# A hybrid decoder layer on one Trainium2 core: the memory branch's norms and roundings are moved into the gates, branch A's first weights are asked for earlier, and softmax scaling goes from VectorE to GpSimd

## The chip, the cores and the metric

One core of one Trainium2 chip runs the whole kernel as one program. Its engines are TensorE (PE, with its weight load PEld), VectorE (DVE), ScalarE (ACT), GpSimd (POOL) and SyncE (SP), which here issues the DMAs. The metric is device microseconds per execution. Lower is better.

## What is computed

One layer of a decoder: a feed-forward block, a mixer of three branches, and a second feed-forward block, on 1024 tokens of width 1024 in f32. Cut to the mixer:

```python
h = rmsnorm(x, mix_norm[l])
z = h @ w_in[l]
u = jax.nn.gelu(z[..., COL_U:COL_V], approximate=False)
v = jax.nn.gelu(z[..., COL_V:COL_CQ], approximate=False)
y_a = spatial_gating(u, v, sg_ln_g[l], sg_ln_b[l], sg_w[l], sg_b[l])
y_b = mla(...)
y_c = memory_attention(z[..., COL_QM:COL_GATE], mem, ...)
gates = jax.nn.sigmoid(z[..., COL_GATE:] + b_gate[l]).reshape(B, S, N_BRANCH, D_MODEL)
merged = (gates[:, :, 0] * (y_a @ w_branch_a[l])
          + gates[:, :, 1] * (y_b @ w_branch_b[l])
          + gates[:, :, 2] * (y_c @ w_branch_c[l]))
...
def memory_attention(q_m, mem, mem_norm, w_kv, q_norm, k_norm):
    q = rmsnorm(q_m.reshape(B, S, MEM_HEADS, MEM_HEAD_DIM), q_norm)
    kv = rmsnorm(mem, mem_norm) @ w_kv
    ...
    s = jnp.einsum('bshd,bmhd->bhsm', q, k).astype(jnp.float32) * (MEM_HEAD_DIM ** -0.5)
    p = jax.nn.softmax(s, axis=-1)
    return jnp.einsum('bhsm,bmhd->bshd', p.astype(v.dtype), v).reshape(B, S, MEM_WIDTH)
```

The memory has 256 rows and the branch has 4 heads of width 128.

## The kernel before

Every f32 operand of a matmul is stored as two parts, `hi` (rounded to fp32r, by ACT) and `lo` (the rest, by DVE): `split` (L129), or `split_gain` (L138) with a gain. A product is three matmuls, hi x hi, hi x lo and lo x hi: `mm3` (L144), whose lines L147 to L149 stand for nearly all of PE's work.

The stages run in this order: feed-forward 1, the gates, the mixer, feed-forward 2. Feed-forward and gates form their products with seven multiplications of half blocks in place of eight. In the gates, `Gates.run` (L1538) goes over units f = 3 to 13. A unit (`unit_steps`, L1338) fetches 1 MB of weights, makes four sums of them on DVE (L1305), splits them (L135, L136) and runs seven products of 12 matmuls. Its four results go through `emit` (L1521): units 0 to 11 give 24 sigmoid gates, units 12 and 13 the four heads of the memory branch's queries, unrounded, and each goes to DRAM from a `raw` buffer.

The mixer is `latent` and `qkv` (branch B's inputs), then `sgu` (L614, branch A up to its projection), then `mem_kv` (L719) and `mem_attention` (L781) of branch C. Inside `sgu`, for the second half of the tokens, `mem_norm` (L690) loads, norms and splits the memory rows between the steps of the U product, and `mem_queries` (L750) loads the four heads into `raw` buffers, squares them (L764), splits them with their gain and leaves the sums over squares (L774) for later. `branches` (L552) is a generator: each step multiplies one 128-column block of branch A's projection for half of the tokens. Its steps serve as filler for PE: three before the first product of `mem_kv`, two before the second, and the rest between the steps of `mem_attention`, where `scores` (S), `turn` (T, transposes) and `value` (V) of eight query tiles follow each other. `scores` ends in minimum, Exp, reciprocal and a scaling on DVE (L806).

What sets the order: in blocks marked `manual_schedule` the named engines keep the written order of the block's instructions. All else is ordered at build time by a list scheduler that simulates the engines: it issues what is ready, with the written order as priority, so work that depends on little is placed early. After that the order of each engine is fixed. In `Gates.run` only PE is named; in `sgu`, `mem_kv` and `mem_attention` no engine is. Buffers come from rings of fixed size by tag, and an instruction that writes a new tile needs a free one: `raw` 3, `whi` and `wlo` 5 each, `h` (`h4`) 16, `x` (`x4`) 10, `w4` 11, `t` (rows) 6; in PSUM `bank` 4, `one` 4 in the gates, `mm` 2 in the mixer. DMAs leave SP's queue in order. In the mixer the sixteen `h4` tiles hold the normed input h until the U products are done.

Of the kernel before, what the change touches and what calls it, by code (L numbers as in the profile page):

```python
# [8 lines left out]
F32 = mybir.dt.float32  # L9
# [7 lines left out]
P = 128  # L17
# [28 lines left out]
class Kernel:  # L46
# [551 lines left out]
    def gelu_rows(self, dst, h, w, pairs, amid={}):  # L598


        gelu = lambda d, x: self.nc.scalar.activation(d, x, ACT.Gelu)
        ps = [self.mm() for _ in range(2)] if pairs else [self.bank() for _ in range(4)]
        for d in range(DT):
            then = amid[d]() if d in amid else None
            for i in range(4):
                b = ps[i // 2][:, i % 2] if pairs else ps[i]
                first = self.mm3(b, tuple(x[:, i * P:(i + 1) * P] for x in h[d]), w[d], d == 0, d == DT - 1)
                if then:
                    self.after(first, then)
                then = None  # L610
        for i, b in enumerate(ps):
            gelu(dst[:, 2 * i:2 * i + 2] if pairs else dst[:, i], b)

    def sgu(self, h):  # L614
        nc, a, tc = self.nc, self.a, self.tc
        with tc.tile_pool(name="sgu", bufs=1) as p:
# [12 lines left out]
            for hf in range(2):  # L629
                vhi, vlo = (p.tile([P, 4, SGW], F32R, name=n, bufs=2) for n in ("v_hi", "v_lo"))  # L630
# [41 lines left out]
        return yt, next(mem), queries  # L672
# [17 lines left out]
    def mem_norm(self):  # L690
# [3 lines left out]
        views = lambda ts: [t[:, i].rearrange("p (c m) -> p c m", m=ML)[:, c]  # L694
                            for t in ts for i in range(2) for c in range(2)]
        x4 = [self.h4() for _ in range(2)]
        x = views(x4)
        for n, t in enumerate(x4):
# [3 lines left out]
        for n in range(4):  # L702
            acc = self.norm_feed(acc, x4[n // 2][:, n % 2], 512)
        nc.vector.tensor_tensor(acc[:, :ML], acc[:, :ML], acc[:, ML:], op=ALU.add)
        yield
        room = lambda: self.mm()[:, 0]
        ss = self.token_sums(acc[:, :ML], late=True, bank=room)
        last = self.final
        r = self.rms(ss, ML // P, D)
        yield last  # L710
        scale = self.norm_scale(r, late=True, bank=room)
        last = self.final
        hi, lo = (views([self.h4(F32R) for _ in range(2)]) for _ in range(2))
        for c in range(DT):
            self.norm_put(hi[c], lo[c], x[c], self.g_mem[:, c:c + 1], scale)
        yield last
        yield hi, lo

    def mem_kv(self, p, mt, fill, amid):  # L719
# [3 lines left out]
        kt = tuple(p.tile([P, MH, ML], F32R, name=n) for n in ("mk_hi", "mk_lo"))  # L723
        vv = tuple(p.tile([P, 2, MH * MD], F32R, name=n) for n in ("mv_hi", "mv_lo"))
# [12 lines left out]
        x = p.tile([P, 2, MH, MD], F32, name="m_k")  # L737
# [3 lines left out]
        amid()  # L741
# [8 lines left out]
    def mem_queries(self):  # L750


        nc = self.nc
        gq = self.stat("m_gq", 1)
        nc.gpsimd.tensor_scalar(gq, self.mq_g, -MD ** -0.5, None, op0=ALU.mult)
        qt, ss = [], []
        for pair in range(MH // 2):
            sq = [self.wide(n).bitcast(F32) for n in ("whi", "wlo")]
            for o in range(2):
                q = self.raw()  # L760
                nc.sync.dma_start(q, self.z[ZQ + 2 * pair + o].rearrange("p a w -> p (a w)"))
                qt.append(self.split_pair(self.h4))
                for n, t in enumerate(sq):
                    nc.scalar.activation(  # L764
                        t[o * P // 2:(o + 1) * P // 2], q[n * P // 2:(n + 1) * P // 2], ACT.Square)
                self.split_gain(*qt[-1], q, gq)
            nc.gpsimd.tensor_tensor(sq[0], sq[0], sq[1], op=ALU.add)
            ss.append(sq[0])
        yield
        b = self.bank()[:, :NT * MH]  # L770
        for pair, sq in enumerate(ss):
            for t in range(NT):
                at = t * MH + 2 * pair
                nc.tensor.matmul(b[:, at:at + 2], sq[:, t * P:(t + 1) * P], self.pick, start=True, stop=True)  # L774
        r = self.const.tile([P, NT * MH], F32, name="mq_r")
        nc.vector.tensor_copy(r, self.rms(b, NT * MH, MD))
        nr = self.const.tile([P, NT * MH], F32, name="mq_nr")
        nc.gpsimd.tensor_scalar(nr, r, -1.0, None, op0=ALU.mult)
        yield qt, r, nr

    def mem_attention(self, p, queries, kt, vv, filler):  # L781

        nc = self.nc
        qt, r, nr = queries
        st = {}

        def scores(i, k):
# [10 lines left out]
            pr = p.tile([P, MH, ML], F32, name="mpr", bufs=3)  # L798
# [7 lines left out]
            nc.vector.tensor_tensor(pr, pr, rs.unsqueeze(2).to_broadcast([P, MH, ML]), op=ALU.mult)  # L806
# [179 lines left out]
    def mixer(self, norm):  # L986
# [12 lines left out]
        ya, mt, queries = self.sgu(h)  # L999
# [9 lines left out]
        branch_a = self.branches(0, ya, sink_a)  # L1009
        with tc.tile_pool(name="mem", bufs=1) as p:  # L1010
            got = []
            kv = self.mem_kv(
                p, mt, lambda n: [next(branch_a) for _ in range(n)], lambda: got.append(next(queries)))
            yc = self.mem_attention(p, got[0], *kv, branch_a)
# [39 lines left out]
    def run(self):  # L1054
# [12 lines left out]
        with tc.tile_pool(name="f1", bufs=1) as fp, self.banks("f1ps") as self.pm:  # L1067
# [45 lines left out]
            self.sig = self.z = gates.z  # L1113
# [391 lines left out]
class Gates(Seven):  # L1505


    def __init__(self, k, w, pool, norm):
        super().__init__(k, w, pool, norm)
        self.z = [k.dram.tile([P, 2, 512], F32, name=f"gate{i}") for i in range(ZB)]  # L1510
        self.o, self.w0 = {}, {}
# [9 lines left out]
    def emit(self, f, i, half, row, ps, into=None):  # L1521
# [12 lines left out]
        o[1] += 1  # L1534
        if o[1] == 2:
            self.nc.sync.dma_start(self.z[n], self.o.pop(n)[0])

    def run(self, x1d, r0):  # L1538
# [3 lines left out]
        last = ZB // 2 - 1  # L1542
        E = mybir.EngineType
        with k.tc.manual_schedule(engines={E.PE}):
            for f in range(3, last + 1):
                self.fetch(f, [x4] * 4 if f % 2 else [x4, w4, x4, w4])
# [8 lines left out]
                self.unit(f)  # L1555
# [426 lines left out]
```

## Time and profile before

| what | value |
|---|---|
| median of 3 runs | 2214.19 us (2213.59 to 2215.88) |
| the profiled execution | 2213.92 us |
| its span, first to last instruction | 2212.1 us |
| mean granted clock of TensorE | 0.997 |
| DMA | 290.12 MB, mean 131 GB/s |
| the gates' units, about | 690 to 930 us of the span |
| `sgu`, about | 1056 to 1140 us |
| `mem_kv` and `mem_attention`, about | 1140 to 1250 us |

A row of groups reads: line of the code, engine, operation, output <- inputs by the program's names, shapes, count | busy us, mean ns of one | idle us of the engine before it and what ended that. A row of the timeline reads: start in us, length in us, engine, line, operation, names, shapes, count of merged instructions, and in brackets the idle time before it and what ended it. A line that is a helper's (L130, L131, L147) stands for many callers, so the tile names tell them apart. Matmul lengths overlap; what a matmul costs is the distance between two starts.

### The profile page before, as it was taken

Reading aid. Unit: us, or ns where it says so; the run is one execution under the profiler, and the core shown is the slowest. Engines: PE = TensorE matmul, PEld = TensorE weight load, DVE = VectorE, ACT = ScalarE, POOL = GpSimd, SP = SyncE. Lnnn points to the kernel's source line nnn. Section 1 sums busy time; section 2 is a strip of 40 time slices with the busy share of each in tenths; the row PEclk is TensorE's granted clock in tenths of the full one; section 3 lists DMA queues with packets and bytes.
Section 4 is the critical chain, followed back from the end, with each engine's and each line's share of the span. In section 5 each row is a group of like instructions: output and inputs, shape, how many; then the busy total and the mean of one; then the engine's idle time right before and its main releaser. Section 6 shows DMA issues by size and latency. Waiting matters only on the chain.

```text
span 2212.1 us, 27569 instructions
## 1 busy us (share of the span) xinstructions
PE 2182.9 (99%) x10280; PEld 1821.0 (82%) x10280; DVE 1548.5 (70%) x2386; ACT 902.0 (41%) x1489; POOL 262.8 (12%) x259
## 2 busy tenths in 40 slices
PE   9999999999999999999989999999999999999999
PEld 5888888888887888898878789988888888888887
DVE  7966666589888555538656668985886666657884
ACT  5422222243455433335435449843442222224332
POOL 2012121100000000003100131140011121210000
PEclk9999999999999999999999999999999999999999
DMA  4242322484432324314424550085032333338543
GB/s 144 81 153 99 103 99 100 162 305 147 148 110 95 115 101 147 110 51 153 129 86 157 211 199 30 30 294 200 29 114 101 100 114 100 115 108 298 174 129 105
DMA packets 114359, 290.12 MB, mean 131 GB/s; under 512 B 13488, under 2 KB 21808, under 8 KB 114224
## 3 DMA queue, kind: packets, MB, share of 16 engines
q1 hardware_dynamic: 114224, 288.36, 37.6%
q8 instruction: 81, 1.33, 0.2%
q14 instruction: 54, 0.44, 0.1%
HBM read 203.90 MB, written 84.41 MB: 130 GB/s over the span
## 4 chain that ended last, share of the span: by engine, by line
PE 89%; DVE 6%; ACT 2%; issue 1%; DMA 1%; POOL 0%; SPq 0%; ACTq 0%; DVEq 0%; POOLq 0%
PE one L147 13%; PE one L148 13%; PE one L149 13%; PE bank L147 13%; PE bank L148 12%; PE bank L149 12%; PE mm L147 2%; PE mm L148 2%; PE mm L149 2%; PE bank L926 1%; PE bank L941 1%; PE bank L942 1%; PE bank L425 1%; DVE wlo L136 1%; DVE wlo L131 1%
## 5 line engine op out<-in xcount | busy, mean ns | idle before, releaser
L135 ACT CAST whi<-x 128x1024 fp32r<-128x1024 f32 (+1 forms) x195 | 185.5, 953 | 489.7 <-PE one L148 215.5
L1332 DVE TENSOR_TENSOR t<-t,one 128x512 f32<-128x512 f32 x182 | 124.9, 686 | 236.3 <-PE one L149 236.1
L147 PE MATMUL bank<-h,whi 128*128 128x512 f32 x660 | 257.1, 390 | 0.0
L148 PE MATMUL bank<-h,whi 128*128 128x512 f32 x660 | 256.9, 389 | 0.0
L149 PE MATMUL bank<-h,wlo 128*128 128x512 f32 x660 | 256.8, 389 | 0.0
L136 DVE TENSOR_TENSOR wlo<-x,whi 128x1024 fp32r<-128x1024 f32 (+1 forms) x195 | 233.0, 1196 | 30.5 <-ACT whi L135 30.4
L147 PE MATMUL one<-h,whi 128*128 128x512 f32 x492 | 193.1, 393 | 0.0
L148 PE MATMUL one<-h,whi 128*128 128x512 f32 x492 | 192.0, 390 | 0.0
L149 PE MATMUL one<-h,wlo 128*128 128x512 f32 x492 | 192.0, 390 | 0.0
L147 PE MATMUL one<-w,whi 128*128 128x512 f32 x408 | 158.7, 389 | 0.0
L148 PE MATMUL one<-w,whi 128*128 128x512 f32 x408 | 158.7, 389 | 0.0
L149 PE MATMUL one<-w,wlo 128*128 128x512 f32 x408 | 158.7, 389 | 0.0
L1726 POOL TENSOR_TENSOR raw<-raw 128x512 f32<-128x512 f32 x38 | 63.0, 1658 | 789.5 <-DVE raw L1581 789.5
L130 ACT CAST whi<-w 128x1024 fp32r<-128x1024 f32 (+1 forms) x108 | 95.1, 899 | 143.9 <-PE one L148 55.2
L131 DVE TENSOR_TENSOR wlo<-w,whi 128x1024 fp32r<-128x1024 f32 (+1 forms) x108 | 110.1, 1033 | 60.5 <-ACT whi L130 60.4
L147 PEld LDWEIGHTS bank<-h,whi 128*128 128x128 f32 x660 | 123.9, 188 | 25.9 <-DVE h L131 0.4
L149 PEld LDWEIGHTS bank<-h,wlo 128*128 128x128 f32 x660 | 123.9, 188 | 25.7
L148 PEld LDWEIGHTS bank<-h,whi 128*128 128x128 f32 x660 | 123.9, 188 | 25.6
L147 PE MATMUL bank<-whi 128*128 128x512 f32 x352 | 136.9, 389 | 0.0
L148 PE MATMUL bank<-wlo,whi 128*128 128x512 f32 x352 | 136.9, 389 | 0.0
L149 PE MATMUL bank<-whi,wlo 128*128 128x512 f32 x352 | 136.9, 389 | 0.0
L148 PEld LDWEIGHTS one<-h,whi 128*128 128x128 f32 x492 | 92.8, 189 | 19.3 <-issue 0.2
(383 smaller groups left out, 4971.6 us busy)
## 6 DMA issues: line engine op xcount, KB each, us to landing
x<-in_ffn_w_gu_dram SPq DMA_DIRECT2D x78, 512.0 KB, 4.8
w<-tdt SPq DMA_DIRECT2D x40, 512.0 KB, 4.6
tdb<-raw SPq DMA_DIRECT2D x64, 256.0 KB, 2.1
h<-in_ffn_w_down_dram SPq DMA_DIRECT2D x64, 256.0 KB, 6.0
w<-tdb SPq DMA_DIRECT2D x30, 512.0 KB, 4.4
gate<-raw SPq DMA_DIRECT2D x27, 512.0 KB, 2.9
tdt<-w SPq DMA_DIRECT2D x48, 256.0 KB, 2.1
tdt<-raw SPq DMA_DIRECT2D x40, 256.0 KB, 2.7
```

What stands on the lines that cost most here:

```text
L130: self.nc.scalar.copy(hi, src)
L131: return (eng or self.nc.vector).tensor_tensor(lo, src, hi.bitcast(F32), op=ALU.subtract)
L135: self.nc.scalar.copy(hi, src)
L136: return lambda: self.nc.vector.tensor_tensor(lo, src, hi.bitcast(F32), op=ALU.subtract)
L147: i = mmul(out, s[0], m[0], start=first, stop=False, **kw)
L148: mmul(out, s[0], m[1], start=False, stop=False, **kw)
L149: self.last = mmul(out, s[1], m[0], start=False, stop=last, **kw)
L425: nc.tensor.transpose(b[:m, k * P:(k + 1) * P], s, self.ident)
L926: nc.tensor.transpose(b[:, at:at + P], prs[t][:, kk * P:(kk + 1) * P], self.ident)
L941: nc.tensor.matmul(o, w, pt[0], start=n == 0, stop=False)
L1332: return self.nc.vector.tensor_tensor(out, x, y, op=ALU.add)
L1726: sub = lambda d, x, y: (eng or nc.gpsimd).tensor_tensor(d, x, y, op=ALU.subtract)
```

## The change

Six edits go together:

1. In `emit`, a query head no longer goes to DRAM as it is. Each finished half is squared into two rows by `fold` (two heads share 128 partitions; the second head's call adds the two rows on GpSimd), and a finished head is split with its gain and stored as two parts, `hi` and `lo`, 512 KB each.
2. `Gates.run` takes the query units 12 and 13 right after unit 4. The sums over squares (`picked`) stand behind the first product of the two units after them, and the inverse roots `mq_r` and `mq_nr` are made at the end of the second.
3. `mem_norm` runs in three steps inside three units (5, 6 and 7), on `x4` buffers, and stores the rounded memory rows as four tiles of parts.
4. `sgu` loads these parts back: memory rows into `h4`, heads 0 and 1 into `h4`, heads 2 and 3 into the tiles that held the first half's V.
5. `branches` loads weights by pairs of blocks, and the first pair is asked for ahead of the second half's U product. An Exp of one column is written behind that product. `sgu`'s pool stays open over the memory attention: keys and values live in `h4`, the softmax tiles (four, before three) in the tiles of the second half's V.
6. The scaling of the softmax rows is on GpSimd.

The matmuls, transposes and sums over tokens are the same ones.

```diff
@@ late_constants
+        self.gq_m = const.tile([P, 1], F32, name="gq_m")
+        nc.gpsimd.tensor_scalar(self.gq_m, self.mq_g, -MD ** -0.5, None, op0=ALU.mult)
@@ branches
+        def weights(d):
+            if d not in w:
+                x = self.load(a["w_branch"][br, d // 2])
+                w[d // 2 * 2], w[d // 2 * 2 + 1] = x[:4], x[4:]
+
+        weights(0)
+        yield
         for n, (dt, hf) in enumerate(steps):
-
             for d, _ in steps[n:n + 2]:
-                if d not in w:
-                    w[d] = self.load(a["w_branch"][br, d // 2][:, d % 2 * 4:d % 2 * 4 + 4])
+                weights(d)
@@ sgu
                 if hf:
-                    mem = self.mem_norm()
-                    next(mem)
-                self.gelu_rows(
-                    u, h[hf], w, hf == 0, {4: lambda: next(mem), 6: lambda: next(mem)} if hf else {})
+                    mt = self.mem_rows()
+                    branch = self.branches(0, yt, sink)
+                    next(branch)
+                self.gelu_rows(u, h[hf], w, hf == 0)
                 if hf:
-                    queries = self.mem_queries()
-                    next(queries)
+                    nc.scalar.activation(self.stat("warm", 1), self.ones, ACT.Exp)
+                    rooms = [v8(n).rearrange("p (a b) w -> p a (b w)", a=2) for n in ("v_hi", "v_lo")]
+                    late = self.mem_queries(1, iter([tuple(x[:, i] for x in rooms) for i in range(2)]))
+                    queries = self.mem_queries(0, iter(lambda: self.split_pair(self.h4), None)) + late
...
-        return yt, next(mem), queries
+            kv = self.mem_kv(mt, lambda n: [next(branch) for _ in range(n)])
+            rooms = [v8(n, F32) for n in ("v_hi", "v_lo")]
+            rooms = [x.rearrange("p (a h) (b m) -> p a (h b) m", a=2, b=2)[:, k] for x in rooms for k in range(2)]
+            return self.mem_attention(queries, rooms, *kv, branch)
@@ mem_norm
+            for d, y in zip(kept[n], (hi, lo)):
+                nc.sync.dma_start(d, y.bitcast(F32))
+
+    def mem_rows(self):
+
+        views = lambda ts: [t[:, i].rearrange("p (c m) -> p c m", m=ML)[:, c]
+                            for t in ts for i in range(2) for c in range(2)]
+        hi, lo = ([self.h4(F32R) for _ in range(2)] for _ in range(2))
+        for n in range(2):
+            for t, src in zip((hi[n], lo[n]), self.mt[n]):
+                self.nc.sync.dma_start(t.bitcast(F32), src)
+        return views(hi), views(lo)
@@ mem_queries
+        out = []
+        for o in range(2):
+            qs = next(rooms)
+            for t, src in zip(qs, self.mq[2 * pair + o]):
+                self.nc.sync.dma_start(t.bitcast(F32), src)
+            out.append(qs)
+        return out
@@ mem_attention
-            pr = p.tile([P, MH, ML], F32, name="mpr", bufs=3)
+            pr = rooms[t % len(rooms)]
...
-            nc.vector.tensor_tensor(pr, pr, rs.unsqueeze(2).to_broadcast([P, MH, ML]), op=ALU.mult)
+            nc.gpsimd.tensor_tensor(pr, pr, rs.unsqueeze(2).to_broadcast([P, MH, ML]), op=ALU.mult)
@@ Gates.emit
+        if n >= ZQ:
+            self.fold(n - ZQ, half, d)
         if o[1] == 2:
-            self.nc.sync.dma_start(self.z[n], self.o.pop(n)[0])
+            t = self.o.pop(n)[0]
+            if n < ZQ:
+                self.nc.sync.dma_start(self.z[n], t)
+            else:
+                qs = k.wide("whi"), k.wide("wlo")
+                k.split_gain(*qs, t.rearrange("p a w -> p (a w)"), k.gq_m)
+                for x, q in zip(qs, self.q[n - ZQ]):
+                    self.nc.sync.dma_start(q, x.bitcast(F32))
+
+    def fold(self, head, half, d):
+
+        nc, o = self.nc, head % 2
+        first = (head // 2, half) not in self.folds
+        if first:
+            self.folds[head // 2, half] = [self.k.row() for _ in range(2)]
+        ts = self.folds[head // 2, half]
+        for i, t in enumerate(ts):
+            nc.scalar.activation(
+                t[o * P // 2:(o + 1) * P // 2], d[i * P // 2:(i + 1) * P // 2], ACT.Square)
+        if not first:
+            nc.gpsimd.tensor_tensor(ts[0], ts[0], ts[1], op=ALU.add)
@@ Gates.run
-        last = ZB // 2 - 1
+        last, queries = ZQ // 2 - 1, (ZQ // 2, ZQ // 2 + 1)
...
-            for f in range(3, last + 1):
-                self.fetch(f, [x4] * 4 if f % 2 else [x4, w4, x4, w4])
+            for n, f in enumerate([3, 4, *queries, *range(5, last + 1)]):
+                self.fetch(f, [x4, w4, x4, w4] if n % 2 else [x4] * 4)
...
-                self.unit(f)
+                steps = self.unit_steps(f)
+                next(steps)
+                if n == 4:
+                    mem = k.mem_norm(self.m)
+                if 4 <= n < 7:
+                    next(mem, None)
+                if n in (3, 4):
+                    if n == 3:
+                        b = k.bank()
+                    self.picked(n - 3, b)
+                for _ in steps:
+                    pass
+                if n == 4:
+                    k.mq_r = k.const.tile([P, NT * MH], F32, name="mq_r")
+                    self.nc.vector.tensor_copy(k.mq_r, k.rms(b[:, :NT * MH], NT * MH, MD))
+                    k.mq_nr = k.const.tile([P, NT * MH], F32, name="mq_nr")
+                    self.nc.gpsimd.tensor_scalar(k.mq_nr, k.mq_r, -1.0, None, op0=ALU.mult)
```

More of the change, by code (lines that the diff above doesn't have):

```diff
@@ L603, in gelu_rows, with sgu @@
         for d in range(DT):
-            then = amid[d]() if d in amid else None
             for i in range(4):
                 b = ps[i // 2][:, i % 2] if pairs else ps[i]
[L607 to L610, printed above, removed]
+                self.mm3(b, tuple(x[:, i * P:(i + 1) * P] for x in h[d]), w[d], d == 0, d == DT - 1)
         for i, b in enumerate(ps):
             gelu(dst[:, 2 * i:2 * i + 2] if pairs else dst[:, i], b)
-    def sgu(self, h):
+    def sgu(self, h, p, sink):
         nc, a, tc = self.nc, self.a, self.tc
-        with tc.tile_pool(name="sgu", bufs=1) as p:
+        v8 = lambda tag, dt=F32R: p.tile([P, 4, SGW], dt, name=tag, tag=tag, bufs=2)
+        if True:
             ln_g = self.bcast_row(p, "ln_g", a["sg_ln_g"], SGW)
@@ L629, in sgu @@
             for hf in range(2):
-                vhi, vlo = (p.tile([P, 4, SGW], F32R, name=n, bufs=2) for n in ("v_hi", "v_lo"))
+                vhi, vlo = (v8(n) for n in ("v_hi", "v_lo"))
                 vs.append((vhi, vlo))
@@ L688, in head_norm, with mem_norm @@
         nc.vector.tensor_tensor(x, x, r.unsqueeze(2).to_broadcast([P, nh, MD]), op=ALU.mult)
-    def mem_norm(self):
+    def mem_norm(self, kept):
         nc, a = self.nc, self.a
[L694 to L698, printed above, removed]
+        x = [self.x4() for _ in range(2)]
+        for n, t in enumerate(x):
             nc.sync.dma_start(
@@ L702, in mem_norm, with mem_kv @@
         for n in range(4):
-            acc = self.norm_feed(acc, x4[n // 2][:, n % 2], 512)
+            acc = self.norm_feed(acc, x[n // 2][:, n % 2], 512)
         nc.vector.tensor_tensor(acc[:, :ML], acc[:, :ML], acc[:, ML:], op=ALU.add)
         yield
[L706 to L719, printed above, removed]
+        r = self.rms(self.token_sums(acc[:, :ML]), ML // P, D)
+        yield
+        scale = self.norm_scale(r)
+        for n, t in enumerate(x):
+            hi, lo = (self.x4(F32R) for _ in range(2))
+            for c in range(4):
+                at = slice(c % 2 * ML, c % 2 * ML + ML)
+                self.norm_put(
+                    hi[:, c // 2, at], lo[:, c // 2, at], t[:, c // 2, at],
+                    self.g_mem[:, 4 * n + c:4 * n + c + 1], scale)
+            for d, y in zip(kept[n], (hi, lo)):
[8 more added lines that the diff above has]
+        return views(hi), views(lo)
+    def mem_kv(self, mt, fill):
         nc, a = self.nc, self.a
-        kt = tuple(p.tile([P, MH, ML], F32R, name=n) for n in ("mk_hi", "mk_lo"))
-        vv = tuple(p.tile([P, 2, MH * MD], F32R, name=n) for n in ("mv_hi", "mv_lo"))
+        kt, vv = (tuple(self.h4(F32R) for _ in range(2)) for _ in range(2))
+        kt = tuple(t.rearrange("p a (b m) -> p (a b) m", b=2) for t in kt)
         def product(w):
@@ L736, in mem_kv @@
         w = self.load(a["mem_w_kv"][1])
-        x = p.tile([P, 2, MH, MD], F32, name="m_k")
+        x = self.h4().rearrange("p a (h d) -> p a h d", h=MH)
         self.head_norm(x, [ps[:, 0], ps[:, 1]])
@@ L748, in mem_kv, with mem_queries, mem_attention @@
         return kt, vv
-    def mem_queries(self):
-        nc = self.nc
[L754 to L784, printed above, removed]
+    def mem_queries(self, pair, rooms):
+        out = []
[5 more added lines that the diff above has]
+        return out
+    def mem_attention(self, qt, rooms, kt, vv, filler):
+        nc = self.nc
+        r, nr = self.mq_r, self.mq_nr
         st = {}
@@ L998, in mixer @@
             self.qkv(*self.latent(h))
-        ya, mt, queries = self.sgu(h)
         def sink_a(d, f, sig, ps):
@@ L1007, in sink_c @@
                 nc.sync.dma_start(mc[d], rows)
[L1009 to L1014, printed above, removed]
+        with tc.tile_pool(name="sgu", bufs=1) as p:
+            yc = self.sgu(h, p, sink_a)
         each = [(d, f) for d in range(DT) for f in range(2)]
@@ L1112, in run @@
             gates.run(x1d, r0)
-            self.sig = self.z = gates.z
+            self.sig, self.mq, self.mt = gates.z, gates.q, gates.m
         with self.banks("mixps") as self.pm:
@@ L1509, in __init__ @@
         super().__init__(k, w, pool, norm)
-        self.z = [k.dram.tile([P, 2, 512], F32, name=f"gate{i}") for i in range(ZB)]
-        self.o, self.w0 = {}, {}
+        self.z = [k.dram.tile([P, 2, 512], F32, name=f"gate{i}") for i in range(ZQ)]
+        self.q = k.dram.tile([MH, 2, P, S], F32, name="mq")
+        self.m = k.dram.tile([2, 2, P, 2, 512], F32, name="mrows")
+        self.o, self.w0, self.folds = {}, {}, {}
     def first(self, f):
```

10 lines of the change are left out of this document (8 added, 2 removed).

## The prediction

> **What bounds the kernel now.** I read the page's head first, then the waits of TensorE (PE; one row is shown: who waited for whom, us in all, times, longest), then a table of windows over the stages that the change touches.
>
> ```profile
> span 2212.1 us, 27569 instructions
> PE 2182.9 (99%) x10280; PEld 1821.0 (82%) x10280; DVE 1548.5 (70%) x2386; ACT 902.0 (41%) x1489; POOL 262.8 (12%) x259
> ```
>
> ```profile
> PE bank L147 <- DVE wlo L131: 2.2, 2, 1.3
> ```
>
> ```profile
> 720.00:760.00 40.00, 40.00 (x178) 33.12 (x177) 22.96 (x31) 15.08 (x20) 0.00 (x0) 1.00 0.38 125
> ...
> 1112.00:1138.00 26.00, 23.87 (x117) 19.86 (x115) 14.25 (x37) 11.98 (x19) 0.79 (x1) 0.93 0.15 45
> 1138.00:1160.00 22.00, 18.32 (x73) 14.69 (x73) 10.69 (x15) 6.29 (x12) 1.57 (x1) 0.92 0.47 162
> ...
> 1192.00:1220.00 28.00, 21.66 (x140) 20.15 (x140) 20.15 (x34) 17.64 (x52) 0.00 (x0) 0.94 0.17 58
> 1220.00:1250.00 30.00, 27.99 (x171) 24.26 (x170) 23.25 (x43) 17.83 (x49) 0.00 (x0) 1.00 0.34 110
> ```
>
> PE is the bound: the change removes none of its matmuls, so it can win only where PE stands still. A window's row holds its length, the busy time of PE, PEld, DVE, ACT and POOL, the granted clock and the DMA. In the gates (720 to 760) PE is never idle. In four windows of the mixer it is idle 2.13, 3.68, 6.34 and 2.01 us. The clock falls there as well: at 0.93, 0.92 and 0.94 it costs 26 x 0.07, 22 x 0.08 and 28 x 0.06, or 1.82, 1.76 and 1.68 us. The four hold 3.95, 5.44, 8.02 and 2.01 us: **19.4 us, 0.9% of the span, is all that there is to win.** How a pause lowers the clock shows here:
>
> ```profile
> 1191.79 0.28 PE L149 MATMUL mm<-mk_hi,h 128*128 128x256 f32 x1
> 1197.14 0.58 PE L147 MATMUL mm<-mk_hi,h 128*128 128x256 f32 x1 [5.07 <-ACT mpr L801]
> 1197.52 0.42 PE L148 MATMUL mm<-mk_lo,h 128*128 128x256 f32 x1
> ```
>
> After a pause of 5.07 us the same matmul takes 0.42 us where it took 0.28.
>
> **Term 1: branch A's weights (window of 1138).**
>
> ```profile
> 1069.72 9.27 SPq L761 DMA_DIRECT2D raw<-gate  x3
> 1135.38 5.63 SPq L96 DMA_DIRECT2D raw<-in_w_branch_dram  x3
> 1140.81 0.62 ACT L130 CAST whi<-raw 128x512 fp32r<-128x512 f32 x1 [1.05 <-DMA raw<-in_w_branch_dram]
> 1141.47 0.50 PE L147 MATMUL bank<-x,whi 128*128 128x512 f32 x1 [3.42 <-ACT whi L130]
> ```
>
> The queries took all three `raw` buffers at 1069.7, and the split that frees them wanted `h4` buffers, so branch A's first load left only at 1135.4. Now queries come back as parts straight into `h4` and `v_hi`/`v_lo` and use no `raw`. The pair of weights is asked for before the last U product, and one `whi`/`wlo` tile holds two d's where a tile held one. I let 5.2 of 5.44 go. Ends: all of it, or nothing, if PE's order puts the first product where something else of it is late.
>
> **Term 2: the second half of SGU (window of 1112).**
>
> ```profile
> 1124.67 3.22 DVE L409 SCALAR_TENSOR_TENSOR h<-h,c_mem_norm,mm 128x256 f32<-128x256 f32 x8 [5.26 <-PE mm L394]
> 1125.18 1.58 ACT L130 CAST h<-h 128x256 fp32r<-128x256 f32 x4 [9.70 <-DVE h L409]
> 1128.67 1.16 ACT L139 ACTIVATE h<-raw,m_gq 128x1024 fp32r<-128x1024 f32 x1
> 1130.16 1.28 DVE L140 SCALAR_TENSOR_TENSOR h<-raw,m_gq,h 128x1024 fp32r<-128x1024 f32 x1
> ```
>
> The memory rows' scaling and splits and the queries' gain splits sat among the Gelus that free PE's banks and among DVE's gating of U. All of them leave. Left are the Gelus themselves; the first half of the same work has 0.30 us of idle PE (1084 to 1112, 27.70 of 28 us). I take 3.0 of 3.95, with ends 1.5 and 3.95.
>
> ```profile
> 1084.00:1112.00 28.00, 27.70 (x141) 23.34 (x140) 19.68 (x54) 10.62 (x16) 1.42 (x1) 1.00 0.19 66
> ```
>
> Twelve 512 KB loads of parts replace six loads here. DMA is at 0.19 and 0.15 in these windows, and `h4` buffers come free as before: covered. If they came late, PE would stand at the scores for their landing (5.7 us for a fetch of this size, by the row on gate weights below).
>
> **Term 3: the first scores (window of 1192).**
>
> ```profile
> 1193.50 1.28 ACT L801 ACT_TABLE_LOAD   x1 [8.91 <-DVE m_mx L797]
> L806 DVE TENSOR_TENSOR mpr<-mpr,m_rs 128x1024 f32<-128x1024 f32 x8 | 9.8, 1225 | 0.2
> L796 DVE TENSOR_REDUCE m_mx<-mm 128x4 f32<-128x1024 f32 x8 | 9.8, 1220 | 2.7 <-PE mm L149 2.6
> L801 ACT ACTIVATE mpr<-mm,m_mx,mq_nr 128x256 f32<-128x256 f32 x32 | 17.8, 576 | 3.2 <-DVE m_mx L797 3.0
> ```
>
> PE waits for a score buffer: two minima in a row on DVE (2.44), a table load (1.28), four Exp (2.2). With the queries' norm ready long before, one minimum can go straight to its Exp: 1.2 us less. The new early Exp would take off 1.28 more, if it ran where it is written. It depends only on `ones`, and nothing holds it. A mixer instruction on a constant already stands at the start of the kernel:
>
> ```profile
> L755 POOL TENSOR_SCALAR m_gq<-c_mem_q_norm x1: 232/232/232, 25.2 to 25.2; 128x1 f32<-128x1 f32 x1
> 4.72 1.15 ACT L1173 ACTIVATE t<-x 128x512 f32<-128x512 f32 x2 [2.42 <-DMA x<-in_x_dram]
> 68.81 1.06 ACT L1585 ACTIVATE raw<-one 128x512 f32<-128x512 f32 x2
> ```
>
> So I expect the early Exp in ACT's first idle 2.42 us: its load is free there, Silu's table must come again before 68.8 (1.28 us on ACT, of which PE feels 0 to 1.3; I take 0.3), and Exp's load stays at 1193. Of the 8.02 I take 3.3 for the shorter chain, its share of the lowered clock and a different order of the fillers, and 1.0 for the pause of 1.27 at 1217 that a DVE split ends. Ends: 0 (a fixed order of PE that again has no filler) and 8.
>
> If ACT takes the early Exp between two Gelus instead, Exp's load and then Gelu's again (1.28 each by the row above) stand there, the second ahead of Gelus that PE waits for: 1.3 us more than my sum, 2202.9. I give that 0.05 of the forecast's chance. The Trainium skill, page "ScalarE: Activation LUTs", section "Table sets: the hidden batching unit", says that functions come in sets and that each change of set is paid with a load, which speaks against a lone Exp among other functions. No run so far shows a switch there and back.
>
> **Term 4: scaling on GpSimd (window of 1220).** DVE has 23.25 of 30 us there and PE waits for its splits. Eight scalings of 1.225 leave it. GpSimd's price is bounded by its rows for the same shape and for half of it:
>
> ```profile
> L767 POOL TENSOR_TENSOR whi<-whi,wlo x2: 2355/2381/2407, 1083.0 to 1137.2; 128x1024 f32<-128x1024 f32 x2
> L591 POOL TENSOR_TENSOR x<-x,x 128x512 f32<-128x512 f32 x16 | 21.4, 1344 | 23.2 <-DVE x L590 21.9 <-DMA x<-md 1.4
> ```
>
> I take 2.38: each tile's chain grows by 1.16. A second tile's scores (1.4), two fillers (12 matmuls at 0.227, 2.7 us each) and later the transposes of the tile before lie between a tile's scores and its own transposes, 6.9 us at the start and about 10 later; the chain (1.22 + 0.2 + 2.2 + 0.2 + 2.38 + some 0.4 of signalling) is 6.6. Hidden, narrowly. I take 1.3 of the 2.01, with ends -9.3 (all eight exposed) and 2.01.
>
> Splits on DVE grow beside GpSimd, as the mean of one form against the same shape elsewhere shows:
>
> ```profile
> L131 DVE TENSOR_TENSOR h<-t,h 128x512 fp32r<-128x512 f32 x8 | 9.3, 1168 | 1.8 <-ACT h L130 1.6
> L131 DVE TENSOR_TENSOR wlo<-h,whi 128x512 fp32r<-128x512 f32 x130 | 88.2, 713 | 26.4 <-ACT whi L130 26.4
> ```
>
> In the softmax most of DVE's inputs are PSUM; only the weights' splits (eight halves of 0.71) have both in SBUF. If each scaling waits for one, 5.7 us come on top of the eight exposed. The Trainium skill, page "SBUF — State Buffer", section "Who interferes with whom", says that a DVE instruction with two SBUF inputs and a GpSimd one that reads SBUF shut each other out for a whole instruction; the two rows agree with it.
>
> **Term 5: what the gates take on.** ACT: 16 squares of 512 columns on half the partitions (two in 1.15 by the row of 4.72), four of memory rows, 4 gain splits of 1.16, 8 casts of 0.40: 9.2 + 2.3 + 4.6 + 3.2 = 19 us. DVE: 4 splits of 1.28, four sums of 0.69, 8 scalings and 8 splits of 0.40: 14 us. POOL: 4 sums of 1.34. SP: eight stores of query parts in place of four, four of memory parts, two loads; DMA is at 0.38. All this falls in five units of 84 x 0.227 = 19.0 us (12 matmuls in the 2.72 us between two rows below), and in every 40 us ACT idles 25 and DVE 17. That covers it; without this room the next unit's casts would come late. Where PE itself waits is at the two sums over squares, put behind a unit's first product:
>
> ```profile
> 790.97 0.39 PE L147 MATMUL bank<-h,whi 128*128 128x512 f32 x1
> 791.17 0.69 DVE L1332 TENSOR_TENSOR raw<-t,one 128x512 f32<-128x512 f32 x1 [1.43 <-PE one L149]
> 793.69 0.39 PE L147 MATMUL one<-w,whi 128*128 128x512 f32 x1
> ```
>
> DVE adds a unit's last product from 791.17 to 791.86; a cast holds ACT to about 792.0, two squares to 793.2, GpSimd's sum to 794.55. PE arrives at 793.69, has the other half's 8 passes to do (0.9 us) and is ready at 794.6: no wait, or 1.2 where GpSimd and a DVE split meet. I take 0.6 twice, 1.2 in all, ends 0 and 2.4. The sums over memory rows and their turn stand a unit behind their inputs: free.
>
> **The sum.** 5.2 + 3.0 + 4.3 + 1.3 - 0.3 - 1.2 = 12.3 us less. The profiled execution took 2213.92 us (span 2212.1 and 1.8 around it; 0.3 below the median of 2214.19): **2201.6**.
>
> **Rivals.** *The softmax keeps its pauses* (10.0 us stay: no filler stands behind the first scores, DVE's relief is eaten by latency): 8.2 - 1.5 = 6.7 less, 2207. For it: PE's order is fixed before the run, and one late Exp stopped it. Against: DVE is freed.
>
> *GpSimd is exposed* at every tile, 8 x 1.16 = 9.3 back: 2211, no change; with the 5.7 of lockouts too, 2216.6, still within what is no change (0.03 of this rival's chance). For it: the margin of 0.3 at the first tile; against: longer cover later.
>
> *Slower: memory rows starve the gates of `x` buffers.* Of ten, four hold T4's parts for the whole stage, and neighbouring units take four and two. The two memory tiles and four parts must come out of the same six, so the fetches of the three units around them can leave late.
>
> ```profile
> x<-in_w_gate_dram SPq DMA_DIRECT2D x18, 512.0 KB, 5.7
> 778.25 0.68 DVE L1305 TENSOR_TENSOR x<-x,x 128x512 f32<-128x512 f32 x1
> 781.33 1.23 DVE L136 TENSOR_TENSOR wlo<-x,whi 128x1024 fp32r<-128x1024 f32 x1
> ```
>
> A fetch needs 5.7 to land, four sums 2.7, cast 1.05 and split 1.23: 10.7 us. The next unit's first parts are ready at 782.6, 8.4 ahead of use at 790.97. A buffer that comes more than 8.4 late stops PE; three units at about 8 are 24 us: 2226. Against: buffers are freed early in a unit of 19 us.
>
> **Chances.** Forecast 0.60 (its own range 2194 to 2208), first rival 0.14, second 0.10, third 0.16. A measurement here tells about 0.2%, 4.4 us, from nothing. Faster 0.74, same 0.10, slower 0.16. The range runs from 2194, where nearly all of the 19.4 is won, to 2215, beyond the second rival; the third and a little below are left out.
>
> **What would show it.** No `raw<-gate` loads, and no wait of PE for branch A's `whi` near 1138; no scaling on DVE and eight on POOL near 2.4 us; a wait of PE for L801 below 4 us; seven table loads with Exp first near 2 us; PE in the gates idle under 2.4 us. Wrong is: a gap in the gates over 5 us, or PE waiting for the transposes of every tile.

## The result, and the profile after

The changed kernel takes 2219.03 us (median of 12 runs, 2215.27 to 2223.24) where the kernel before takes 2214.43 (12 runs, 2213.46 to 2217.47): a ratio of 1.0019, 95% interval 1.0010 to 1.0028. It is not faster; if anything it is 0.2% slower. The profiled execution took 2216.38 us, one of the shorter ones. Its head and TensorE's waits in the gates, from 720 to 910 us (who waited for whom, us in all, times, longest):

```profile
span 2214.7 us, 27600 instructions
PE 2183.5 (99%) x10280; PEld 1820.2 (82%) x10280; DVE 1537.4 (69%) x2378; ACT 904.4 (41%) x1499; POOL 277.9 (13%) x269
```

```profile
PE bank L147 <- ACT whi L135: 8.4, 2, 4.2
PE one L147 <- DVE raw L1322: 1.2, 1, 1.2
PE bank L149 <- DVE wlo L136: 1.1, 2, 0.8
PE one L147 <- DVE t L1322: 0.5, 1, 0.5
```

In the kernel before, TensorE waits for nothing in this window. The tables of windows say how much was won and lost, stage by stage. First the kernel before: the gates, the end of SGU with the start of branch A, the softmax, the rest of the mixer (length, then busy us of PE, PEld, DVE, ACT and POOL, the granted clock, the DMA).

```profile
720.00:910.00 190.00, 190.00 (x842) 157.36 (x841) 105.37 (x136) 69.22 (x90) 0.00 (x0) 1.00 0.35 119
1090.00:1160.00 70.00, 63.88 (x301) 52.92 (x300) 38.62 (x88) 24.77 (x39) 2.35 (x1) 0.95 0.22 72
1160.00:1300.00 140.00, 131.65 (x716) 113.59 (x716) 86.90 (x162) 56.15 (x146) 23.46 (x23) 0.99 0.59 209
1300.00:1500.00 200.00, 197.97 (x1290) 177.87 (x1289) 177.16 (x346) 149.86 (x327) 51.90 (x101) 1.00 0.33 123
```

The same windows of the changed kernel:

```profile
720.00:910.00 190.00, 178.80 (x785) 146.11 (x784) 107.34 (x163) 78.37 (x108) 5.42 (x5) 0.97 0.39 137
1090.00:1160.00 70.00, 69.70 (x337) 58.58 (x336) 41.21 (x106) 21.98 (x35) 0.00 (x0) 1.00 0.49 162
1160.00:1300.00 140.00, 134.36 (x716) 115.26 (x715) 75.70 (x142) 53.19 (x142) 36.20 (x28) 0.99 0.56 200
1300.00:1500.00 200.00, 198.20 (x1298) 178.54 (x1297) 176.13 (x346) 149.28 (x325) 53.31 (x102) 1.00 0.33 120
```

Read as in the prediction (idle time of PE plus length times what is missing of the clock), the end of SGU falls from 6.12 + 3.5 to 0.30 us, 9.3 won. The two windows behind it fall from 8.35 + 2.03 to 5.64 + 1.80 of idle time at the same clock, to the two digits shown: 2.9 won. The gates rise from nothing to 11.20 + 190 x 0.03, **16.9 lost**. That is 4.7 lost on balance. The medians are 4.6 apart, but the two profiled executions, from which the rows come, only 2.5; these windows do not place the other 2.2. The mixer won most of what was hoped, and the gates took back more than that.

Where in the gates? Here is ScalarE's (ACT's) order of time in the changed kernel around the end of the first unit with queries, then TensorE at the starts of the units behind the two query units (start, duration, engine, line, operation; in brackets the engine's idle time before and who ended it).

```profile
767.42 1.27 ACT L1547 ACTIVATE t<-raw 64x512 f32<-64x512 f32 x2 [4.22 <-DVE raw L1322]
770.14 1.28 ACT L1547 ACTIVATE t<-raw 64x512 f32<-64x512 f32 x2 [1.45 <-DVE raw L1322]
771.44 1.15 ACT L139 ACTIVATE whi<-raw,gq_m 128x1024 fp32r<-128x1024 f32 x1
772.86 1.27 ACT L1547 ACTIVATE t<-raw 64x512 f32<-64x512 f32 x2 [0.27 <-DVE raw L1322]
774.15 1.15 ACT L139 ACTIVATE whi<-raw,gq_m 128x1024 fp32r<-128x1024 f32 x1
775.21 1.98 ACT L135 CAST whi<-x 128x1024 fp32r<-128x1024 f32 x2
777.09 1.56 ACT L135 CAST whi<-w 128x1024 fp32r<-128x1024 f32 x2
```

```profile
776.29 0.79 PE L147 MATMUL bank<-h,whi 128*128 128x512 f32 x1 [4.19 <-ACT whi L135]
...
804.43 0.50 PE L147 MATMUL bank<-h,whi 128*128 128x512 f32 x1 [4.19 <-ACT whi L135]
```

The next unit's four weight casts (L135) start at 775.21, behind the last gain split of the queries (L139). ACT idles 4.22 us a little earlier, so it is not out of time; it was given the casts in this place. TensorE waits 4.19 us for the first of them, in each of the two units. The first matmul behind the wait takes 0.79 us in one and 0.50 in the other, where 0.39 is its usual time.

### The profile page after: what moved, and what is told of

Read it like the earlier page. It is cut to its first block, busy times and chain, and to the rows that moved or that the text cites. A ratio compares the mean times of both kernels' runs of the same rounds, so it can differ in the third digit from the quotient of the medians.

```text
span 2214.7 us, 27600 instructions
## 1 busy us (share of the span) xinstructions
PE 2183.5 (99%) x10280; PEld 1820.2 (82%) x10280; DVE 1537.4 (69%) x2378; ACT 904.4 (41%) x1499; POOL 277.9 (13%) x269
## 4 chain that ended last, share of the span: by engine, by line
PE 90%; DVE 5%; ACT 3%; DMA 1%; issue 1%; POOL 0%; ACTq 0%; SPq 0%; DVEq 0%; POOLq 0%
PE one L147 13%; PE one L148 13%; PE one L149 13%; PE bank L147 13%; PE bank L149 13%; PE bank L148 13%; PE mm L147 2%; PE mm L149 2%; PE mm L148 2%; PE bank L921 1%; PE bank L936 1%; PE bank L427 1%; PE bank L937 1%; DVE wlo L136 1%; DMA x<-in_w_gate_dram 1%
## 5 line engine op out<-in xcount | busy, mean ns | idle before, releaser
L135 ACT CAST whi<-x 128x1024 fp32r<-128x1024 f32 (+1 forms) x195 | 185.0, 953 | 474.9 <-PE one L148 199.4
L131 DVE TENSOR_TENSOR wlo<-w,whi 128x1024 fp32r<-128x1024 f32 (+1 forms) x108 | 110.2, 1034 | 61.0 <-ACT whi L130 60.9
L149 PEld LDWEIGHTS one<-h,wlo 128*128 128x128 f32 x492 | 92.8, 189 | 19.3
```

Source lines behind the costliest of these rows:

```text
L131: return (eng or self.nc.vector).tensor_tensor(lo, src, hi.bitcast(F32), op=ALU.subtract)
L135: self.nc.scalar.copy(hi, src)
L149: self.last = mmul(out, s[1], m[0], start=False, stop=last, **kw)
```

## The experiments

Theory A, formed from these rows: the parts of the query heads take two `whi`/`wlo` buffers at the end of a unit, and the code asks for them *before* it asks for the next unit's weights out of the same ring of five. Who asks later is placed later in ACT's and DVE's order. Theory B: squares and parts are too much work for ACT and DVE there. Each run is set beside runs of the kernel before on the same chip.

**The same work, asked for later (defer).**

```
# emit, n >= ZQ, instead of the split and the stores:
self.owed.append((n, t))
# run:
steps = self.unit_steps(f)
next(steps)        # the next unit's first two weights and its first product
self.parts()       # wide("whi"), wide("wlo"), split_gain, two stores, as before
```

> The changed kernel, but the query heads' parts are claimed and written after the next unit's first two weight casts have been issued, with the same instructions and the same five whi/wlo buffers. Theory A (order of claims: the two whi/wlo buffers of the parts are claimed ahead of the next unit's weights, which share that ring, so ACT and DVE are given the casts only behind the parts): the two pauses of 4.6 us near 772 and 800 us go, the excess of TensorE over its step in 720 to 905 falls from 16.6 to under 4 us, PE's wait for the whi cast falls from 8.4 us to under 1, and the time from 2219.0 to about 2206 (2203 to 2209). Theory B (squares and parts are simply too much work for ACT and DVE at that place): the pauses stay or move, the excess stays over 10 us, and the time is within 3 of 2219.

2202.0 us (2201.83 to 2203.12) against 2214.68; ratio 0.9945, 0.9932 to 0.9959. ACT's order in defer, and windows of it:

```profile
762.18 1.05 ACT L135 CAST whi<-x 128x1024 fp32r<-128x1024 f32 x1 [4.67 <-PE bank L148]
...
763.75 1.28 ACT L1553 ACTIVATE t<-raw 64x512 f32<-64x512 f32 x2
```

```profile
760.00:800.00 40.00, 40.00 (x193) 33.68 (x192) 23.23 (x30) 23.47 (x33) 5.14 (x4) 1.00 0.45 165
```

```profile
720.00:910.00 190.00, 188.66 (x850) 156.37 (x849) 114.56 (x172) 83.31 (x114) 5.46 (x5) 1.00 0.40 142
1160.00:1300.00 140.00, 133.35 (x730) 114.95 (x728) 74.28 (x141) 55.11 (x149) 40.36 (x34) 0.99 0.51 183
1300.00:1500.00 200.00, 199.22 (x1277) 178.78 (x1276) 172.53 (x333) 144.19 (x313) 50.22 (x96) 1.00 0.37 138
```

The casts stand in ACT's idle time again, ahead of the squares. ACT does 23.47 us of work between 760 and 800, and TensorE is never idle there: B falls. The gates' loss goes from 16.9 to 1.34 us, and the median falls by 17.0, more than A's 13; the two profiled executions, the changed kernel's being a short one, are 13.6 apart.

**The requests alone, without the work (claim), and their control (claim_late).** The kernel before, with two extra buffers of each kind asked for at the end of two units, one column written into each.

```
+ if n in (10, 11, 12, 13):
+     hi, lo = k.wide("whi"), k.wide("wlo")
+     self.nc.scalar.copy(hi[:, :1], t[:, 0, :1])
+     self.nc.vector.tensor_copy(lo[:, :1], t[:, 0, :1])
```

> The kernel before, in which two units of the gates each end with two extra claims of a whi and a wlo buffer, with one column cast into each; no squares, no parts, nothing else. Theory A (order of claims): the next unit's four weight casts stand behind these claims on ACT, PE pauses 2 to 4.6 us at the start of the unit after each, with a lowered clock behind it, and the time rises from 2214.4 to 2218 to 2225. Theory B (amount of work): four columns cost nothing, PE has no pause over 1 us there, the time stays within 1 of 2214.4.

> The control for claim: the kernel before with the same extra claims and the same single columns, asked for only behind the next unit's first two weights. Theory A (order of claims): no pause over 0.5 us between 720 and 910 us, and the time is that of the kernel before within 1.5 us. Theory B (two more whi/wlo buffers in use at the border of two units are too many, in any order): the pauses of 1.5 us stay or come later in the unit, and the time is 2 to 5 us over the kernel before.

claim: 2218.57 us against 2214.68; ratio 1.0017, 1.0008 to 1.0026. claim_late: 2215.03 against 2214.5; ratio 1.0000, 0.9991 to 1.0009. ACT in claim, then TensorE's only wait in the gates and their window in claim, then that window in claim_late:

```profile
772.10 0.28 ACT L1540 CAST whi<-raw 128x1 fp32r<-128x1 f32 x2
772.29 1.99 ACT L135 CAST whi<-x 128x1024 fp32r<-128x1024 f32 x2
774.19 1.56 ACT L135 CAST whi<-w 128x1024 fp32r<-128x1024 f32 x2
```

```profile
PE bank L149 <- DVE wlo L136: 2.2, 2, 1.1
720.00:910.00 190.00, 187.64 (x825) 154.11 (x824) 101.17 (x133) 68.05 (x92) 0.00 (x0) 1.00 0.34 116
```

```profile
720.00:910.00 190.00, 190.00 (x841) 157.30 (x841) 105.25 (x140) 69.04 (x94) 0.00 (x0) 1.00 0.35 119
```

In each of the two units two columns that cost ACT 0.28 us push four whole casts behind them, and TensorE loses 2.36 us in all; the wait on record is for DVE's part `wlo` of the first weight, which is made from that cast. The same columns asked for one product later cost nothing. A pause of claim is some 1.2 us, shorter than A's 2 to 4.6, since nothing but the requests stands ahead of the casts; in the changed kernel the parts' own work stands there too. Of the 3.9 us that claim costs, 2.36 lie in the gates, and no row here places the rest.

**Other rings for the parts (ownx4, ownx).** The changed kernel with `k.split_pair()` (x buffers) or `k.split_pair(self.w4)` in place of `k.wide("whi"), k.wide("wlo")`.

> The changed kernel with the query heads' parts in x buffers in place of whi/wlo. Theory A (order of claims, in whichever ring the parts and the next unit's weights share): the next unit's x buffers (its sums' rooms) are claimed behind the parts, its casts need those sums, so they stay behind the parts on ACT: the pauses of 3 to 5 us near 772 and 800 stay and the time is 2217 to 2222. Theory B (only the count of whi/wlo buffers matters): whi and wlo have all their five again, the pauses go, the time is near 2206.

> The changed kernel with the query heads' parts in w4 buffers, of which the next unit claims two (its third and fourth weights) but none for its first and second weights' casts. Theory A: the first cast stands ahead of the parts again, since no claim of its own stands behind theirs, so the pause at the start of the unit goes; the second one needs a sum whose room is a w4 claimed behind the parts and comes late, so that a pause of 1 to 4 us stays, one product later; 2207 to 2216. Theory B (count of buffers): no pause at all, near 2206.

ownx4: 2229.97 us against 2215.14, ratio 1.0064 (1.0049 to 1.0080). ownx: 2217.01, ratio 1.0005 (0.9996 to 1.0014). TensorE, ACT and the DMA queue in ownx4, then TensorE and DVE in ownx:

```profile
783.62 0.79 PE L147 MATMUL bank<-h,whi 128*128 128x512 f32 x1 [9.93 <-ACT whi L135]
782.52 1.04 ACT L135 CAST whi<-x 128x1024 fp32r<-128x1024 f32 x1 [5.64 <-DMA x<-in_w_gate_dram]
774.20 3.03 SPq L1537 DMA_DIRECT2D mq<-x  x3
777.28 0.45 SPq L1278 DMA_DIRECT2D x<-in_w_gate_dram  x1
```

```profile
785.77 0.79 PE L147 MATMUL one<-w,whi 128*128 128x512 f32 x1 [9.33 <-ACT whi L135]
782.75 0.69 DVE L1295 TENSOR_TENSOR w<-x,w 128x512 f32<-128x512 f32 x1 [6.25 <-DMA w<-in_w_gate_dram]
```

B came out in neither: five `whi`/`wlo` buffers for the weights alone do not help. What shares the ring with the parts is late, whichever ring it is. In x and w4 that is not only a cast but a fetch, which leaves behind stores of the parts and then needs its time to land, so a pause is 9.3 to 10.8 us where the cast's was 4.2 (twice in ownx4; once in ownx, and why its second unit with queries is spared is not shown). Theory A had the places right, the second product in ownx among them, and the sizes too small: the fetch was missing from it, and with it ownx4's time was missed by 8 us and ownx's by 1. No run makes the ring of `whi`/`wlo` larger, so whether two more buffers would have removed the pauses as well stays open.

**The pause that is left (defer_lo).** In defer the gates still lose 1.34 us, at 851. DVE and TensorE there:

```profile
849.48 0.69 DVE L1295 TENSOR_TENSOR w<-x,w 128x512 f32<-128x512 f32 x1 [2.85 <-DMA x<-in_w_gate_dram]
852.68 0.50 PE L147 MATMUL one<-x,whi 128*128 128x512 f32 x1 [1.34 <-DVE raw L1322]
```

A unit's sums wait for a weight fetch that left late. The edit gives the memory rows two buffers less:

```
- hi, lo = (self.x4(F32R) for _ in range(2))
+ hi, lo = self.x4(F32R), t.bitcast(F32R)
```

> As defer, but the memory rows' low parts are written over the rows themselves, so that the norm claims four x buffers where it claimed six. Theory A (the one pause left in the gates, 1.7 us at 851, comes from a weight fetch that waits for an x buffer behind the memory rows' stores): PE's wait of 1.3 us for raw goes, the excess between 840 and 880 us falls from 1.7 to under 0.5, and the time is 1 to 2 us under defer's 2202.0. Theory B (the sixteen scalings and splits on DVE, 6.1 us in one block, are what is late): pause and time stay within 0.5 of defer.

2201.66 us against 2215.14; ratio 0.9940, 0.9927 to 0.9952. The window of the gates in defer_lo:

```profile
720.00:910.00 190.00, 189.59 (x854) 157.25 (x853) 115.63 (x174) 84.35 (x115) 5.48 (x5) 1.00 0.41 142
```

TensorE's idle time there falls from 1.34 to 0.41 us and its wait for `raw` is gone, as A had it. The 1 to 2 us that A expected of the time did not come: it is 0.3 under defer, which ran on another chip, within the spread of both.

**The weights of branch A, undone and alone (defer_lazy, ahead).** defer_lazy is defer without `weights(0); yield` and without `next(branch)`. ahead is the kernel before with these lines alone, asked for in front of the queries.

> As defer, but branch A's first weights are loaded and cast where the kernel before does it, when the branch begins. Theory A (the prediction's term of 5.2 us): PE waits again some 3.7 us for the whi cast at the start of branch A, with a lowered clock behind it, and the time is 5 us over defer's 2202.0 (4 to 6). Theory B (the time it wins is lost again at the next wait): 0 to 2 us over defer.

> The kernel before, in which branch A's first weights alone are loaded and cast ahead, in front of the queries, as the change has it; queries and memory rows stay in the mixer. Theory A (the place of the weights is what wins the prediction's 5.2 us at the start of branch A): PE's pause of 3.7 us near 1138 goes, the pauses of the spatial products before it (1.2, 0.7, 0.9 us) stay, and the time falls from 2214.4 by 4 to 5 to about 2210. Theory B (the queries' reads and squares, which take raw and whi/wlo buffers and time of ACT ahead of the weights, are what makes them late; defer_lazy showed that without the queries there the place is free): the pause only moves to another weight or the next read, and the time falls by under 2 us.

defer_lazy: 2202.11 us against 2215.14, 0.1 over defer (on another chip). ahead: 2212.04 against 2215.36; ratio 0.9988, 0.9979 to 0.9997. The window of SGU's end in defer_lazy, then that of ahead, TensorE's new wait there and what DVE does ahead of it:

```profile
1090.00:1160.00 70.00, 69.70 (x345) 58.76 (x344) 38.25 (x91) 22.68 (x38) 0.00 (x0) 1.00 0.55 184
```

```profile
1090.00:1160.00 70.00, 63.81 (x299) 52.72 (x298) 40.23 (x79) 30.48 (x45) 4.75 (x2) 0.93 0.22 76
```

```profile
PE bank L147 <- DVE x L131: 2.5, 1, 2.5
```

```profile
1138.33 2.30 DVE L140 SCALAR_TENSOR_TENSOR h<-raw,m_gq,h 128x1024 fp32r<-128x1024 f32 x1 [1.05 <-ACT h L139]
1140.56 2.47 DVE L131 TENSOR_TENSOR x<-bank,x 128x512 fp32r<-128x512 f32 x4
```

Asking for the weights ahead is not what wins this window. Without it the window stays full; with it alone PE idles 6.19 us as before, waiting 2.5 us for the transposed U (DVE L131) where it waited for the weight. That leaves the queries' and memory rows' work, which is gone from the mixer in defer_lazy: in ahead a query's gain split of 2.30 us (L140) stands right ahead of the split that TensorE waits for. The two were not taken out one by one. The 3.3 us that ahead does win, between A's 4 to 5 and B's under 2, lie elsewhere, and no run here places them.

**GpSimd's scaling (defer_dve, gps).** One word: `nc.gpsimd` back to `nc.vector` in defer, and the reverse in the kernel before.

> As defer, but the softmax rows are scaled on DVE again, as in the kernel before. Theory A (the scaling on GpSimd is hidden and takes DVE's time off the path, the prediction's term of 1.3 us): 1.3 us slower than defer, 0.5 to 2.6. Theory B (2.4 us on GpSimd is late for the transposes of some tiles): 1 to 3 us faster than defer, and PE's waits for the scaled rows shrink.

> The kernel before, with the scaling of the softmax rows on GpSimd alone. Theory A (the term as defer_dve measured it): 2 to 3 us under 2214.4, about 2212. Theory B (as the prediction had it): 1.3 us under, about 2213. Theory C (in the older kernel the first rows meet other waits, so that 2.4 us on GpSimd are exposed): at or over 2214.4.

defer_dve: 2204.86 us (2203.32 to 2206.21), 2.9 over defer. gps: 2213.0 against 2215.36; ratio 0.9989, 0.9980 to 0.9998, 2.4 less. Four of the eight scalings of the changed kernel on GpSimd, then the windows of the softmax and of the rest of the mixer in defer_dve:

```profile
L801 POOL TENSOR_TENSOR v_lo<-v_lo,m_rs 128x1024 f32<-128x1024 f32 x4 | 7.6, 1896 | 12.2 <-DVE m_rs L800 12.2
```

```profile
1160.00:1300.00 140.00, 131.86 (x717) 113.45 (x716) 80.65 (x145) 53.23 (x144) 24.84 (x24) 0.99 0.51 184
1300.00:1500.00 200.00, 198.87 (x1279) 178.42 (x1278) 174.20 (x336) 145.95 (x316) 50.38 (x98) 1.00 0.37 135
```

Two comparisons from two sides agree: it is worth 2.4 to 2.9 us. The 1.3 of the prediction and of defer_dve's theory A (at most 2.6) were too small.

**The early Exp, held in its place (defer_exp, lo_exp).**

```
- nc.scalar.activation(self.stat("warm", 1), self.ones, ACT.Exp)
+ nc.scalar.activation(self.stat("warm", 1), u[:, 3, :1], ACT.Exp)
```

> As defer, and the early Exp reads one column of the last Gelu's result, so that it can't stand ahead of it. Theory A (the table load of 1.28 us at the first softmax lies on the path): five table loads for six, the one for Exp stands behind the last Gelu near 1120 us, PE's wait for the first softmax's Exp falls from 3.5 to about 2.2 us, the time is 1.3 us under defer. Theory B (the softmax's max or scaling ends that wait, not the load): the wait and the time stay as in defer within 0.5.

> defer_lo with the Exp's table load behind the last Gelu as in defer_exp. Theory A (the 1.1 us that defer_exp's PE won at the first scores are real and were hidden by the spread of its runs): 2200.5, five table loads. Theory B (they are lost again at a later wait): 2201.7, as defer_lo.

defer_exp: 2202.87 us (2199.59 to 2203.89) against defer's 2202.0. lo_exp: 2200.01 (2199.05 to 2200.57) against 2215.36; ratio 0.9931, 0.9919 to 0.9944. The two waits of TensorE at the first softmax, in the changed kernel and in lo_exp, with lo_exp's table load:

```profile
1201.83 0.58 PE L147 MATMUL mm<-h,h 128*128 128x256 f32 x1 [3.51 <-ACT v_hi L796]
```

```profile
1135.69 1.28 ACT L663 ACT_TABLE_LOAD   x1
1185.56 0.38 PE L147 MATMUL mm<-h,h 128*128 128x256 f32 x1 [2.23 <-ACT v_hi L796]
```

The load leaves the softmax, five loads are left of six, and the wait falls by 1.28 us, the load's own length. The times do not settle what this is worth: nothing in the first pair, 1.7 us in the second, whose two kernels ran on different chips. lo_exp is the fastest kernel of the study, 0.7% under the kernel before.

## Why the prediction was wrong

The forecast was 2201.6 and the time is 2219.0. **The step that failed stands in term 5: "That covers it; without this room the next unit's casts would come late."** The room was there. ACT had 16.5 us of 40 left even in defer, which does the same work in the same stage. What the sum over busy times could not see is the place of that work: the parts were asked for ahead of the next unit's weights in the ring of `whi`/`wlo`, and the casts were put behind them. Priced at 1.2 us, this term cost 16.9, and with the same work asked for later it costs 1.34.

The consequence that the prediction named for the case without room (late casts) is the one that happened, for another reason. How the ring brings it about is inferred: at 775.21 ACT shows no wait for a buffer, since the order was fixed before the run. The runs show that, with five buffers of each kind, the place of the request in the written order decides it; the request and the work on the buffer were always moved together, in claim_late with next to no work.

Step by step:

- *Terms 1 and 2* (8.2 of 9.4): 9.3 won. The size was right. Of the reasons given, the work that leaves SGU stands; that the weights are "asked for before the last U product" does not (defer_lazy, ahead), and the freed `raw` buffers were not tried by themselves.
- *Term 3* (4.3) and *term 4* (1.3): together 2.9 in the changed kernel, 3.0 in defer (8.35 + 2.03 to 6.65 + 0.78 of idle time), where 5.6 were taken. Term 4 was too small (2.4 to 2.9 measured; the scaling takes 1.90 us and not 2.38, which may be why), and term 3 was too large: defer_dve, defer without term 4, has 8.14 + 1.13 us of idle time, so the rest of the change wins 1.1 there of the 4.3. PE's wait at the first softmax fell from 5.07 to 3.51 us, under the 4 named.
- *The early Exp*: as predicted it was drawn to the start of the kernel and the softmax kept its load. But it stands ahead of Silu's first table load, not behind it (ACT's table loads of the changed kernel, below), so Silu's had not to come again: six loads in all, not seven, and the 0.3 us were not spent.

```profile
0.81 1.28 ACT L663 ACT_TABLE_LOAD   x1 [0.81 <-PEq L2009]
2.32 1.28 ACT L209 ACT_TABLE_LOAD   x1
...
1198.18 1.28 ACT L796 ACT_TABLE_LOAD   x1 [6.45 <-DVE m_mx L792]
```

- *Rivals*: GpSimd was not exposed. The softmax kept most of its pauses, as the first rival had it. The slower one had the right kind of mechanism in the wrong ring: the memory rows' x buffers cost 1.3 us once, not 24. The same question put to `whi`/`wlo` would have pointed at the loss.

Of the signs of being wrong, "a gap in the gates over 5 us" would have missed two gaps of 4.19; PE's idle time in the gates, 11.20 us where under 2.4 was expected, shows the loss.

That defer lands at 2202.0, next to the forecast, is partly luck: 1.1 too little in terms 1 and 2 against 2.6 too much in terms 3 and 4.

## What to carry to other kernels

When work moves into a stage, list what it asks for out of each ring of buffers and where in the code's order it asks, next to who asks behind it; free time on the engines does not answer that question. If a moved step shares a ring with the next unit's inputs, let it ask after them: here a change of that order was worth 17 us, while another ring for the moved step won 2 us in one case and lost 11 in the other. A pause at the start of one unit after another is a sign of it. The Trainium skill, page "Perfetto Trace Analysis", section "Optimization Strategy", says that a gap that repeats can mean too few buffers for the next tile. Here claim and claim_late have the same buffers and the same number of requests, and the place of the requests makes the gap (2.36 us of idle time against none); whether more buffers would close it too, no run here shows.

## What was not expected of the hardware

GpSimd scales 128x1024 in 1.90 us, where the sum of two tiles of that shape took 2.38 in the kernel before; the second operand is here one number per 256 columns. And a pause costs more than itself: after the 4.19 us of waiting at 776 the changed kernel's matmuls take 0.63 us for 0.39, and the nine steps from 776.88 to 781.38, with a wait of 0.30 among them, take 4.50 us where 9 x 0.227 is 2.04:

```profile
776.88 0.63 PE L148 MATMUL bank<-h,whi 128*128 128x512 f32 x1
...
781.38 0.49 PE L148 MATMUL bank<-h,whi 128*128 128x512 f32 x1
```

Behind the pause of 1.34 us at 852 in defer the second step is already 0.23 us long again (853.02 to 853.25). Behind the changed kernel's second wait of 4.19 us, at 804.43, the first step takes 0.34 us, and steps of 0.43 come only behind a further wait of 0.79 us; what sets their start is not shown.
